# A different form of the seven-product block pair in an FFN, and a fourth pair in the first FFN

## The chip, the cores and the metric

The kernel runs on one core of one Trainium2 chip. The metric is the device time of one execution in microseconds (us); a kernel's time is the median of its runs. Engines are named as in the profile: PE is TensorE (PEld its weight loads), DVE is VectorE, ACT is ScalarE, POOL is GpSimd, SP is SyncE, which only issues loads. L433 is the line of the profile for nearly every instruction, since a helper (issue, line 430) emits them all.

## The reference

Two layers on 256 tokens of width 1024, everything in float32. Each layer is a macaron half-step FFN, a mixer (an mLSTM in layer 0, a differential attention on a shared K/V in layer 1), a second half-step FFN, and a gated per-layer embedding, each with a norm before and behind it. Four FFNs hence, of this form, with a hidden width of 2816:

```
def swiglu(x, w_in, w_out):
    gate, up = jnp.split(x @ w_in, 2, axis=-1)
    return (jax.nn.silu(gate) * up) @ w_out
...
        h = swiglu(rms_norm(x, g[0]), w_ffn_in[layer, 0], w_ffn_out[layer, 0])
        x = x + 0.5 * rms_norm(h, g[1])
...
        h = swiglu(rms_norm(x, g[4]), w_ffn_in[layer, 1], w_ffn_out[layer, 1])
        x = x + 0.5 * rms_norm(h, g[5])
```

## The kernel before, in words

The 256 tokens are two tiles of 128 (NT = 2). An FFN (function ffn) is cut into 11 items (NJ) of 256 hidden columns, gate and up together 512 columns. An item's input weight is two tiles of 128x2048 float32, 1 MB each, its output weight is one such tile. Each tile is loaded into one of NRAW = 10 buffers `wraw` and split in two (split, line 464): ACT copies the high part into one of NPART = 6 buffers `whi`, DVE subtracts to get the low part into one of NLOW = 5 buffers `wlo`. A float32 product of 128 rows is then three matmuls (mm3, line 507): high by high, high by low, low by high. So stage_in(j, t), the input product of item j for token tile t, is 24 matmuls of 128x512; hidden(j, t) makes silu(gate) times up, transposes it on PE and splits it; stage_out(j, t) adds 12 matmuls into the output sum.

A block pair (block_pair, line 718) does two items for both token tiles with 7 products of 12 matmuls where single items need 8: it is a 2x2 block scheme of the Winograd kind. Its names: src is the first item's two weight tiles (b11, b21), src2 the second's (b12, b22); xf gives four sums of the token side, s1, s2, s3 and n4 (forms, line 700). On the weight side it needs t3 = b12 + b22 and u1 = b11 + b12, which a second, accumulating transfer on POOL's queue adds to a loaded tile (load with plus), and wt2 = b11 + t3 and wt4 = b21 + wt2, which DVE adds. w11, w21, w22, wu1, wt2, wt3, wt4 are the split forms. The products in order are x0·w11, x0·w21 (together p1, hidden(0, 0)), s2·wt2, s1·wu1 (held as z5), s3·wt3, n4·w22, x1·wt4, and use(item, t, source) hands each finished sum to hidden. Here b22 is loaded by itself for w22, beside the t3 that holds it already, so a pair loads 5 tiles and accumulates 2. For a pair that follows a pair of the same FFN, t3 and u1 are loaded a pair ahead (ahead, nxt). Behind a pair come the stage_outs of the items before it.

PAIRS names the items at which pairs start: (5, 7, 9) in the first FFN, (1, 3, 5, 7, 9) in the other three, so 18 pairs; the mLSTM has 2 more. Items 3 and 4 of the first FFN are single.

The order of the work is no more than partly that of the code. The program is written down first (Notes), then a planner (play, line 267) takes for each engine the next operation by its costs, a rank from the program's order and whether the operation is marked urgent, gives the buffers, and issue emits each engine's operations in that order. On the chip every engine then works strictly in its own order and waits for semaphores.

## Time and profile before

| | |
|---|---|
| runs of the kernel | 1003.70, 1004.13, 1004.54 us; median 1004.13 |
| the profiled execution | 1002.59 us |
| its span in the trace | 1000.8 us |
| granted PE clock, mean | 0.997 |
| moved by DMA | 274.68 MB |

The span runs from the first to the last instruction in the trace; 1.8 us of the profiled time lie around it. The FFNs take, by the order of the stages, the first part (0 to about 150 us), from about 280, from about 500, and the end from about 780 us on. Busy times of engines are shares of the span; an engine that waits for a semaphore is idle in them. A matmul's listed length is modelled and reaches over the start of the next one, so the distance from start to start is what it costs.

### The profile page before, as it was taken

How to read it: one execution, taken by the hardware profiler on the slowest of the kernel's cores; microseconds unless marked ns; L12 is line 12 of the kernel's file. 1: busy time of each engine (PE TensorE's matmuls, PEld its weight loads, DVE VectorE, ACT ScalarE, POOL GpSimd, SP SyncE). 2: the span in 40 equal slices, each digit the busy share in tenths (PEclk: the TensorE clock that was granted, in tenths of full speed). 3: DMA queues.
4: the chain of work that ended last, by engine and by line, in shares of the span. 5: the costliest groups of instructions: out<-in, count | busy, mean ns of one | idle time of the engine just before them, and what ended most of it. 6: DMA issues, size and time to landing. Idle time of an engine off the chain costs nothing.

```text
span 1000.8 us, 12442 instructions
## 1 busy us (share of the span) xinstructions
PE 986.4 (99%) x4636; PEld 803.0 (80%) x4636; DVE 892.8 (89%) x909; ACT 698.6 (70%) x924; POOL 94.9 (9%) x126
## 2 busy tenths in 40 slices
PE   9999999999999999999999999999999999999997
PEld 7888888887787778888878888888888887878786
DVE  6977999799999999998799999898984999999983
ACT  7746777578756877685867767686776776757752
POOL 0010000300141000001120000001002300000010
PEclk9999999999999999999999999999999999999998
DMA  9999948765699999765699999864759899996621
GB/s 345 420 339 343 311 179 296 244 207 198 255 320 340 326 309 335 279 247 207 261 301 330 324 353 347 329 244 161 253 210 285 235 297 318 313 295 252 242 84 43
DMA packets 45859, 274.68 MB, mean 274 GB/s; under 512 B 5480, under 2 KB 5864, under 8 KB 16104
## 3 DMA queue, kind: packets, MB, share of 16 engines
q1 hardware_dynamic: 39752, 231.69, 60.2%
q0 software_dynamic: 5760, 41.95, 20.6%
q8 instruction: 36, 0.59, 0.2%
q10 hardware_dynamic: 288, 0.27, 0.1%
q14 instruction: 23, 0.19, 0.1%
HBM read 263.40 MB, written 10.49 MB: 274 GB/s over the span
## 4 chain that ended last, share of the span: by engine, by line
PE 47%; issue 2%; ACT 2%; POOL 1%; DVE 1%; DVEq 0%; POOLq 0%; ACTq 0%
PE accI L433 30%; PE accO L433 15%; PE tr L433 2%; POOL sm L433 1%; ACT sg L433 1%; DVE wlo_4r L433 0%; ACT att L433 0%; DVE wlo_2r L433 0%; ACT wraw L433 0%; ACT whi_5r L433 0%; ACT whi_0r L433 0%; DVE wraw L433 0%; DVE att L433 0%; DVE xl_5r L433 0%; DVEq L1498 0%
## 5 line engine op out<-in xcount | busy, mean ns | idle before, releaser
L433 DVE TENSOR_TENSOR wraw<-wraw,wraw 128x2048 f32<-128x2048 f32 x40 | 91.4, 2284 | 0.1
L433 ACT ACTIVATE whi_1r<-wraw 128x2048 fp32r<-128x2048 f32 (+2 forms) x49 | 72.7, 1494 | 18.2 <-PE accI L433 8.8
L433 ACT ACTIVATE whi_4r<-wraw 128x2048 fp32r<-128x2048 f32 (+1 forms) x45 | 75.4, 1684 | 11.9 <-issue 4.4
L433 ACT ACTIVATE whi_2r<-wraw 128x2048 fp32r<-128x2048 f32 (+1 forms) x48 | 79.4, 1661 | 5.5 <-issue 2.6
L433 ACT ACTIVATE whi_5r<-wraw 128x2048 fp32r<-128x2048 f32 (+1 forms) x47 | 79.2, 1694 | 5.6 <-PE accI L433 4.7
L433 ACT ACTIVATE whi_0r<-wraw 128x2048 fp32r<-128x2048 f32 (+2 forms) x48 | 74.5, 1557 | 6.8 <-PE accI L433 3.4
L433 ACT ACTIVATE whi_3r<-wraw 128x2048 fp32r<-128x2048 f32 (+1 forms) x45 | 73.6, 1647 | 3.3 <-PE accI L433 1.6
L433 ACT ACTIVATE att<-accI 128x512 f32<-128x512 f32 x80 | 47.5, 594 | 38.1 <-PE accI L433 37.8
L433 POOL DMA_DIRECT2D wraw<-in_ffn_in x36 | 32.0, 889 | 343.5 <-DMA wraw<-in_ffn_in 286.3
L433 POOL TENSOR_SCALAR sm<-sm 128x1 f32<-128x1 f32 x32 | 23.5, 735 | 308.8 <-ACT sg L433 308.8
L433 POOL TENSOR_TENSOR sm<-sm,mhalf 128x1 f32<-128x1 f32 (+2 forms) x40 | 30.7, 769 | 108.2 <-DVE sm L433 105.6
L433 ACT ACTIVATE sg<-att,sm 128x256 f32<-128x256 f32 x54 | 26.9, 502 | 16.9 <-DVE att L433 16.8
L433 ACT ACTIVATE sg<-accO 128x512 bf16<-128x512 f32 (+2 forms) x46 | 20.2, 445 | 25.0 <-PE accO L433 21.0
L433 ACT ACTIVATE sg<-accI,sm 128x256 f32<-128x256 f32 x34 | 16.0, 470 | 29.3 <-PE accI L433 27.3
L433 PEld LDWEIGHTS tr<-ident,sg 128*128 128x128 f32 x176 | 23.0, 140 | 14.6 <-DVE hl_2r L433 2.7
L433 PE MATMUL tr<-ident,sg 128*128 128x128 f32 x176 | 34.0, 274 | 0.3 <-DVE hl_2r L433 0.3
L433 DVE SCALAR_TENSOR_TENSOR wraw<-wraw,sm,wraw 128x512 f32<-128x512 f32 x32 | 22.7, 749 | 12.0 <-POOL sm L433 11.9
L433 DVE TENSOR_TENSOR att<-accI,att 128x512 f32<-128x512 f32 x40 | 27.4, 685 | 3.3 <-PE accI L433 2.9
L433 ACT ACTIVATE sg<-wraw 128x512 bf16<-128x512 f32 x32 | 20.1, 630 | 13.7 <-DVE wraw L433 9.7
L433 ACT ACTIVATE att<-accI,sm 128x512 f32<-128x512 f32 (+1 forms) x22 | 14.8, 671 | 20.8 <-PE accI L433 20.8
L433 DVE SCALAR_TENSOR_TENSOR sg<-att,sm,sg 128x256 f32<-128x256 f32 x54 | 25.7, 480 | 1.7 <-ACT sg L433 1.5
L433 DVE TENSOR_TENSOR att<-att,att 128x512 f32<-128x512 f32 (+1 forms) x33 | 22.4, 679 | 3.8 <-ACT att L433 3.6
(610 smaller groups left out, 3249.9 us busy)
## 6 DMA issues: line engine op xcount, KB each, us to landing
wraw<-in_ffn_in SPq DMA_DIRECT2D x102, 1024.0 KB, 9.4
wraw<-in_ffn_out SPq DMA_DIRECT2D x44, 1024.0 KB, 8.3
wraw<-in_ffn_in POOLq DMA_DIRECT2D x36, 1024.0 KB, 13.3
wraw<-in_mlstm_in SPq DMA_DIRECT2D x14, 1024.0 KB, 5.3
wraw<-in_ple_gate SPq DMA_DIRECT2D x8, 1024.0 KB, 5.1
wraw<-in_w_kv SPq DMA_DIRECT2D x8, 1024.0 KB, 4.8
home<-wraw SPq DMA_DIRECT2D x28, 256.0 KB, 5.1
wraw<-home SPq DMA_DIRECT2D x14, 512.0 KB, 5.4
```

The lines of the kernel that those rows point to most:

```text
L433: getattr(getattr(self.nc, eng), name)(*args, **kw)
```

## The change

NRAW goes from 10 to 9 and NLOW from 5 to 6, which takes the same room. PAIRS gives the first FFN a fourth pair, items 3 and 4; as the first pair of its FFN it has the old form, and pair (5, 6) now follows a pair. Every pair that follows another of its FFN (15 of them now) takes a new form, the branch `if ahead is not None`; the first pairs of the four FFNs and the two of the mLSTM keep the old one.

In the new form only u1 is loaded a pair ahead. The tile for t3 is loaded with b22 alone and split for w22, and then an accumulating transfer adds b12 into the same buffer, which makes it t3; so b22 isn't loaded a second time (4 loads and 2 accumulates). The products are in another order: s1·wu1 and n4·w22 first (both held in pieces, z5 and z4, one ACT copy more), then x0·w11 and x0·w21, then the stage_outs of the items before, which stood behind the pair (between, outs), and then s2·wt2, s3·wt3 and x1·wt4. In the last pair of an FFN one stage_out is kept for behind it.

```
-NRAW = 10
+NRAW = 9
 NPART = 6
-NLOW = 5
+NLOW = 6
...
-PAIRS = ((5, 7, 9),) + ((1, 3, 5, 7, 9),) * 3
+PAIRS = ((3, 5, 7, 9),) + ((1, 3, 5, 7, 9),) * 3
...
+        if ahead is not None:
+            nc.is_urgent = False
+            u1 = ahead
+            t3 = load(src2[1])
+            nc.is_urgent = True
+            w22 = parts(t3)
+            nc.gpsimd.dma_start(t3, src2[0], accum_op=ALU.add)
+            nc.is_urgent = False
+            wu1 = parts(u1)
+            b11 = load(src[0])
+            w11 = parts(b11)
+            b21 = load(src[1])
+            w21 = parts(b21)
+            nc.is_urgent = True
+            s1, s2, s3, n4 = xf() if callable(xf) else xf
+            az = acc_in()
+            times(az, s1, wu1, False)
+            z5 = held(az)
+            times(az, n4, w22, True)
+            z4 = held(az)
+            ax, ay = acc_in(), acc_in()
+            times(ax, quarter(0, 0), w11, False)
+            p1 = held(ax)
+            times(ay, quarter(0, 4), w21, False)
+            nc.vector.tensor_tensor(p1, ay, p1, op=ALU.add)
+            use(0, 0, p1)
+            if between:
+                between()
+            nc.is_urgent = False
+            wt2 = add(b11, b11, t3)
+            ahead = load(nxt[0][0], nxt[1][0]) if nxt else None
+            wt3 = parts(t3)
+            wt4 = add(b21, b21, b11)
+            nc.is_urgent = True
+            times(ax, s2, wt2, True)
+            u2 = held(ax)
+            nc.vector.tensor_tensor(u2, z4, u2, op=ALU.subtract)
+            use(1, 0, u2)
+            times(ax, s3, wt3, True)
+            u3 = held(ax)
+            nc.vector.tensor_tensor(z5, z5, u3, op=ALU.subtract)
+            use(1, 1, z5)
+            times(ax, quarter(1, 4), wt4, True)
+            use(0, 1, ax)
+            return ahead
         nc.is_urgent = False
-        t3, u1 = ahead or (load(src2[0], src2[1]), load(src[0], src2[0]))
+        t3, u1 = load(src2[0], src2[1]), load(src[0], src2[0])
...
-        ahead = (load(nxt[1][0], nxt[1][1]), load(nxt[0][0], nxt[1][0])) if nxt else None
+        ahead = load(nxt[0][0], nxt[1][0]) if nxt else None
...
             if len(item) == 2:
                 nxt = items[begin + n + 1]
-                ahead = both(item, between=late if split_begin and n == 0 else None, ahead=ahead,
-                             nxt=[win[i] for i in nxt] if len(nxt) == 2 else None)
+                between = late if split_begin and n == 0 else (lambda: outs(behind)) if ahead is not None else None
+                ahead = both(item, between=between, ahead=ahead, nxt=[win[i] for i in nxt] if len(nxt) == 2 else None)
...
-            both(item, end=True, ahead=ahead)
...
+            both(item, end=True, between=lambda: outs(behind, 1), ahead=ahead)
+            outs(behind)
```

How this moves instructions is shown at three places. In these rows a name such as wraw_3_79 is buffer 3 of `wraw`, a row "wlo<-wraw,whi" is the low half of a split, a row "wraw<-wraw,wraw" an add of two weight tiles, and "att" and "sg" rows are the small ones on held sums and hidden values.

The first place is DVE at the meeting of the first and the second pair of the fourth FFN. Before, the last row is the split of the second pair's u1 (wraw_3_79); ahead of it stand the splits of the first pair's wt4 (wraw_7_83) and of the second pair's b21 (wraw_4_80) and the add of its wt2 (wraw_0_76). The split of the first pair's wt2 lies nine rows above the first one shown:

```order
L433 TENSOR_TENSOR att_4_102<-att_4_102,att_6_104 128x512
L433 TENSOR_TENSOR wlo_1r_72<-wraw_7_83,whi_4r_69 128x2048
L433 TENSOR_TENSOR att_1_99<-accI_0_90,att_1_99 128x512
L433 SCALAR_TENSOR_TENSOR sg_0_126<-att_4_102,sm1_5_161,sg_0_126 128x256
L433 TENSOR_TENSOR wlo_3r_74<-wraw_4_80,whi_3r_68 128x2048
L433 TENSOR_TENSOR hl_0r_123<-tr_0_97,hh_0r_120 128x256
L433 SCALAR_TENSOR_TENSOR sg_1_127<-att_1_99,sm1_6_162,sg_1_127 128x256
L433 SCALAR_TENSOR_TENSOR sg_2_128<-accI_1_91,sm1_5_161,sg_2_128 128x256
L433 TENSOR_TENSOR wraw_0_76<-wraw_0_76,wraw_8_84 128x2048
L433 TENSOR_TENSOR hl_1r_124<-tr_0_97,hh_1r_121 128x256
L433 TENSOR_TENSOR att_3_101<-accI_0_90,att_3_101 128x512
L433 TENSOR_TENSOR wlo_2r_73<-wraw_3_79,whi_5r_70 128x2048
```

In the changed kernel the rows begin with the split of the first pair's wt2 (wraw_2_79) and end with that of the second pair's u1 (wraw_3_80); w22 of the second pair (wraw_1_78) is among them:

```order
L433 TENSOR_TENSOR wlo_4r_75<-wraw_2_79,whi_2r_67 128x2048
L433 TENSOR_TENSOR xl_6r_119<-att_4_102,xh_6r_112 128x512
L433 TENSOR_TENSOR wlo_1r_72<-wraw_7_84,whi_4r_69 128x2048
L433 SCALAR_TENSOR_TENSOR sg_0_126<-accI_2_92,sm1_5_161,sg_0_126 128x256
L433 TENSOR_TENSOR wlo_5r_76<-wraw_6_83,whi_0r_65 128x2048
L433 TENSOR_TENSOR wlo_4r_75<-wraw_1_78,whi_2r_67 128x2048
L433 TENSOR_TENSOR hl_0r_123<-tr_0_97,hh_0r_120 128x256
L433 TENSOR_TENSOR wlo_0r_71<-wraw_0_77,whi_5r_70 128x2048
L433 TENSOR_TENSOR wlo_2r_73<-wraw_4_81,whi_3r_68 128x2048
L433 TENSOR_TENSOR att_3_101<-att_3_101,att_6_104 128x512
L433 TENSOR_TENSOR wlo_1r_72<-wraw_3_80,whi_4r_69 128x2048
```

So from wt2 of the first pair to u1 of the second there lie seven operations on whole weight tiles (128x2048), both counted, and four small rows; before, ten and eleven. The splits of b11 and b21 and the add of wt2 of the second pair have moved behind u1, the add of the first pair's wt4 to ahead of these rows, and w22 of the second pair has come in.

The second place is DVE a little later in the same pair, before with the splits of wt2, t3 and b22, the add of wt4 (wraw_4_80) and then the first of the output weights (wraw_6_82, in two halves):

```order
L433 SCALAR_TENSOR_TENSOR sg_0_126<-att_3_101,sm1_6_162,sg_0_126 128x256
L433 TENSOR_TENSOR wlo_0r_71<-wraw_0_76,whi_0r_65 128x2048
L433 TENSOR_TENSOR wlo_1r_72<-wraw_8_84,whi_1r_66 128x2048
L433 TENSOR_TENSOR wlo_4r_75<-wraw_1_77,whi_4r_69 128x2048
L433 TENSOR_TENSOR wraw_4_80<-wraw_4_80,wraw_0_76 128x2048
L433 TENSOR_TENSOR wlo_2r_73<-wraw_6_82,whi_3r_68 128x1024
L433 TENSOR_TENSOR att_5_103<-att_5_103,att_7_105 128x512
L433 TENSOR_TENSOR wlo_2r_73<-wraw_6_82,whi_3r_68 128x1024
L433 TENSOR_TENSOR att_0_98<-accI_1_91,att_0_98 128x512
```

In the changed kernel, behind u1, come b11 (wraw_5_82), b21 (wraw_8_85), the two output weights (wraw_2_79 and wraw_7_84), and only then the add of wt2, which takes t3 from wraw_1_78:

```order
L433 SCALAR_TENSOR_TENSOR sg_1_127<-att_3_101,sm1_5_161,sg_1_127 128x256
L433 TENSOR_TENSOR wlo_3r_74<-wraw_5_82,whi_1r_66 128x2048
L433 TENSOR_TENSOR hl_2r_125<-tr_0_97,hh_2r_122 128x256
L433 SCALAR_TENSOR_TENSOR sg_2_128<-att_1_99,sm1_6_162,sg_2_128 128x256
L433 SCALAR_TENSOR_TENSOR sg_0_126<-accI_1_91,sm1_5_161,sg_0_126 128x256
L433 TENSOR_TENSOR wlo_5r_76<-wraw_8_85,whi_0r_65 128x2048
L433 TENSOR_TENSOR hl_0r_123<-tr_0_97,hh_0r_120 128x256
L433 TENSOR_TENSOR wlo_0r_71<-wraw_2_79,whi_5r_70 128x1024 x2
L433 TENSOR_TENSOR wlo_2r_73<-wraw_7_84,whi_3r_68 128x2048
L433 TENSOR_TENSOR wraw_5_82<-wraw_5_82,wraw_1_78 128x2048
```

The output weights have moved ahead of wt2, t3 and wt4, as the stage_outs have on PE; the add of wt2 stands behind six whole splits and one in two halves and eight small rows, counted from w22's. The two halves of one output weight lie in one row of the order ("x2").

The third place is POOL in the first FFN, before with its six accumulating transfers for three pairs, two by two:

```order
L433 DMA wraw_7_83<-in_ffn_in 128x2048 [waits DMAHW7_49]
L433 DMA wraw_8_84<-in_ffn_in 128x2048 [waits DMAHW0_49]
L433 DMA wraw_3_79<-in_ffn_in 128x2048 [waits DMAHW5_49,DMAHW6_49,DMAHW4_49,DVE_49]
L433 DMA wraw_4_80<-in_ffn_in 128x2048 [waits DMAHW5_49]
L433 DMA wraw_8_84<-in_ffn_in 128x2048 [waits DMAHW3_49]
L433 DMA wraw_7_83<-in_ffn_in 128x2048 [waits DMAHW4_49]
```

In the changed kernel there are eight for four pairs:

```order
L433 DMA wraw_2_79<-in_ffn_in 128x2048 [waits DMAHW3_49,DMAHW1_49,DMAHW4_49,DMAHW0_49,DVE_49]
L433 DMA wraw_3_80<-in_ffn_in 128x2048 [waits DMAHW5_49,DMAHW6_49,DMAHW1_49,DVE_49]
L433 DMA wraw_7_84<-in_ffn_in 128x2048 [waits DMAHW7_49]
L433 DMA wraw_1_78<-in_ffn_in 128x2048 [waits DMAHW1_49,DVE_49]
L433 DMA wraw_4_81<-in_ffn_in 128x2048 [waits DMAHW6_49]
L433 DMA wraw_8_85<-in_ffn_in 128x2048 [waits DMAHW7_49,DVE_49,Activation_49]
L433 DMA wraw_1_78<-in_ffn_in 128x2048 [waits DMAHW4_49]
L433 DMA wraw_4_81<-in_ffn_in 128x2048 [waits DMAHW0_49,DVE_49]
```

Of each later pair one of the two transfers, the one that makes t3, now waits for DVE to have split the tile it goes into, and stands on POOL's queue ahead of or behind the other pair's u1 as shown.

More of the change, by code (lines that the diff above doesn't have):

```diff
@@ L712, in forms, with load @@
         return [q1, q2, q3, q4]
-    def block_pair(xts, xf, src, src2, use, end=False, between=None, nxt=None, ahead=None):
-        def load(src, plus=None):
-            raw = T([P, 2048], "wraw", NRAW)
-            nc.sync.dma_start(raw, src)
-            if plus is not None:
-                nc.gpsimd.dma_start(raw, plus, accum_op=ALU.add)
-            return raw
+    def load(src, plus=None):
+        raw = T([P, 2048], "wraw", NRAW)
+        nc.sync.dma_start(raw, src)
+        if plus is not None:
+            nc.gpsimd.dma_start(raw, plus, accum_op=ALU.add)
+        return raw
+    def block_pair(xts, xf, src, src2, use, end=False, between=None, nxt=None, ahead=None):
         def parts(raw):
@@ L762, in held @@
             return c
+        if ahead is not None:
[43 more added lines that the diff above has]
+            return ahead
+        nc.is_urgent = False
+        t3, u1 = load(src2[0], src2[1]), load(src[0], src2[0])
+        b11 = load(src[0])
+        w11 = parts(b11)
+        b21 = load(src[1])
+        w21 = parts(b21)
+        wt2 = add(b11, b11, t3)
+        wu1 = parts(u1)
+        wt3 = parts(t3)
+        b22 = load(src2[1])
+        w22 = parts(b22)
+        ahead = load(nxt[0][0], nxt[1][0]) if nxt else None
+        wt4 = add(b21, b21, b11)
+        nc.is_urgent = True
         ax, ay = acc_in(), acc_in()
@@ L871, in late, with outs @@
             stage_out(0, 1)
+        def outs(todo, keep=0):
+            while len(todo) > keep:
+                stage_out(*todo.pop(0))
         def all_forms():
@@ L889, in ffn @@
                     stage_in(item[0], t)
-            for t in range(NT):
-                for i in last:
-                    stage_out(i, t)
+            outs(behind)
             last = item
@@ L908, in ffn @@
         else:
-            both(item, end=True, ahead=ahead)
-            for t in range(NT):
-                for i in last:
-                    stage_out(i, t)
+            behind = [(i, t) for t in range(NT) for i in last]
+            both(item, end=True, between=lambda: outs(behind, 1), ahead=ahead)
+            outs(behind)
             for t in range(NT):
```

13 lines of the change are left out of this document (1 added, 12 removed).

## Prediction

> **What bounds the kernel now.** I read the page first, then the windows by stretch, then the chain of waits and the timelines where a window showed a gap. The page's busy times, and one piece of the chain from the third FFN (start us, us, what):
>
> ```profile
> PE 986.4 (99%) x4636; PEld 803.0 (80%) x4636; DVE 892.8 (89%) x909; ACT 698.6 (70%) x924; POOL 94.9 (9%) x126
> 593.25 15.90 PE accI L433 x70
> ```
>
> TensorE is the bound: 99% of the span. Its unit price is in the second line: 70 matmuls of 128x512 in 15.90 us, 0.227 us each, so a product or a stage_out of 12 costs 2.72 us. VectorE (DVE) at 89% is the only other engine that can decide, and the mean hides where. Windows of 30 us (start:end, window's length, then PE, PEld, DVE, ACT, POOL busy, granted clock, DMA share, GB/s), the first two in the second FFN, one in the third, two in the fourth:
>
> ```profile
> 300.00:330.00 30.00, 28.88 (x130) 22.41 (x129) 29.61 (x31) 22.27 (x27) 4.41 (x6) 1.00 1.02 354
> 330.00:360.00 30.00, 29.38 (x131) 23.10 (x130) 30.00 (x26) 22.92 (x26) 1.72 (x2) 1.00 0.99 307
> 600.00:630.00 30.00, 30.00 (x137) 24.57 (x136) 29.89 (x22) 20.82 (x22) 1.72 (x2) 1.00 1.02 330
> 830.00:860.00 30.00, 27.67 (x124) 21.96 (x123) 29.53 (x24) 20.09 (x21) 1.74 (x2) 1.00 0.97 309
> 860.00:890.00 30.00, 30.00 (x135) 24.07 (x134) 28.54 (x22) 20.86 (x22) 1.73 (x2) 1.00 0.99 314
> ```
>
> In the pairs DVE is 95 to 100% busy and TensorE full, except at the starts of the second and fourth FFN, where PE falls short by 1.12 + 0.62 and 2.33 us while DVE is full: there DVE decides. The chain at the start of the fourth FFN, and PE's timeline in the second (in brackets the idle time before a matmul and its releaser):
>
> ```profile
> 829.82 0.69 DVE att L433
> 830.51 2.21 DVE wlo_2r L433
> 832.72 0.04 issue
> ...
> 838.28 0.61 ACT att L433
> ```
> ```profile
> 313.11 0.39 PE L433 MATMUL accI<-whi_5r,xh_2r 128*128 128x512 f32 x1
> 314.15 0.50 PE L433 MATMUL accI<-wlo_4r,xh_2r 128*128 128x512 f32 x1 [0.65 <-DVE wlo_4r L433]
> ...
> 317.17 0.38 PE L433 MATMUL tr<-ident,sg 128*128 128x128 f32 x2
> 318.02 0.50 PE L433 MATMUL accI<-whi_4r,xh_4r 128*128 128x512 f32 x1 [0.47 <-ACT att L433]
> ```
>
> The piece of 2.21 us is DVE's low part of u1 of the second pair, which TensorE stands and waits for: 0.69 + 2.21 there and 0.61 later, about 3.5 us on the chain, of which the window shows 2.33 as idle. The profiled run took 1002.59 us (span 1000.8), 1.54 less than the median 1004.13, so I work against 1002.59 and add 1.54 at the end.
>
> **The change, part by part.**
>
> *One more pair in the first FFN.* Items 3 and 4 go from 8 products to 7: 12 matmuls x 0.227 = 2.7 us less of TensorE. This holds in full only if nothing else becomes late.
>
> *What the new pair asks of the first FFN.* Two single items need 4 splits of 128x2048; a pair in the old form, which this one is, as the first of its FFN, has 7 splits and 2 adds, so 5 DVE operations more. Their price, DVE's timeline in the fourth FFN, and the room, windows of 25 us and ACT's waits for loads between 25 and 100 us (total, times, longest):
>
> ```profile
> 833.02 2.29 DVE L433 TENSOR_TENSOR wlo_0r<-wraw,whi_0r 128x2048 fp32r<-128x2048 f32 x1
> 835.23 2.29 DVE L433 TENSOR_TENSOR wlo_1r<-wraw,whi_1r 128x2048 fp32r<-128x2048 f32 x1
> ```
> ```profile
> 50.00:75.00 25.00, 25.00 (x115) 20.60 (x114) 18.03 (x15) 10.58 (x11) 3.04 (x4) 1.00 1.02 339
> 75.00:100.00 25.00, 25.00 (x114) 20.60 (x113) 19.74 (x16) 17.45 (x18) 1.80 (x3) 1.00 1.02 342
> 100.00:125.00 25.00, 25.00 (x114) 20.59 (x113) 23.98 (x19) 17.85 (x17) 0.00 (x0) 1.00 1.00 313
> ```
> ```profile
> ACT whi_4r L433 <- DMA wraw<-in_ffn_out: 0.6, 1, 0.6
> ACT whi_3r L433 <- DMA wraw<-in_ffn_in: 0.6, 1, 0.6
> ```
>
> From one start to the next is 2.20 us, so 11.0 us, and three small operations on held pieces of about 0.7 make 13. DVE idles 25 - 18.03 and 25 - 19.74, 12.2 us together, from 50 to 100. So it just about fits, and DVE will be full there. The DMA share is full too (1.02). The page's queue rows price a load:
>
> ```profile
> q1 hardware_dynamic: 39752, 231.69, 60.2%
> q0 software_dynamic: 5760, 41.95, 20.6%
> ```
>
> 60.2% of 1000.8 us over 231.69 MB is 2.6 us per MB on the 16 engines, and 20.6% over 40 accumulating MB is 5.15 us. The new pair has 5 loads and 2 accumulates against 4 loads: 2.6 + 10.3 = 12.9 us more; the three pairs behind it each drop one load, 7.8 us less. Net 5.1 us in a stage whose loads now land with hardly a wait (0.6 us on ACT, none on PE). The cost is between 0 (cover found behind the leads and in the sixth low buffer) and about 6 us (half of the 12.9 comes through before the three pairs give it back). I take 1.5, near the low end, since PE's windows there are full, 25.00, and DVE's demand exceeds its idle time by only about 1 us.
>
> *The new product order in 15 pairs.* DVE work per pair stays the same (7 splits, 2 adds, and the outs), so a pair that is not at a start gains nothing. What changes is when DVE must deliver. In the old order 7 products (19.0 us of PE) stand together and need 9 whole-tile operations of DVE (19.8 us) and the small ones; in the new one 4 products and 4 stage_outs (21.8 us) need 4 + 2 splits (13.2 us) and the small ones, and the other five (11.0 us) serve three products behind those outs. So DVE is short of time in the old order, which it makes up in the outs, and ahead in the new. The case to work is the fourth FFN (the order pieces above show it): from DVE's split of the first pair's wt2 to that of the second pair's u1. DVE's timeline has them at
>
> ```profile
> 804.59 2.28 DVE L433 TENSOR_TENSOR wlo_1r<-wraw,whi_2r 128x2048 fp32r<-128x2048 f32 x1
> ...
> 819.82 0.69 DVE L433 TENSOR_TENSOR att<-att,att 128x512 f32<-128x512 f32 x1 [0.27 <-ACT att L433]
> ...
> 825.82 0.42 DVE L433 TENSOR_TENSOR hl_0r<-tr,hh_0r 128x256 fp32r<-128x256 f32 x1
> ...
> 830.43 2.28 DVE L433 TENSOR_TENSOR wlo_2r<-wraw,whi_5r 128x2048 fp32r<-128x2048 f32 x1
> ```
>
> Before, ten whole-tile operations lie from the one to the other, both counted, and it ends at 832.6. In the changed order seven lie there with four small ones (0.4 to 0.7 each, as above), 7 x 2.20 + 2.0 = 17.4 us: it could end at 822.0, or, since the small operation at 819.82 waits for ACT and stands just ahead, at 819.82 + 0.6 + 2.2 = 822.6. TensorE wants it now first in the pair instead of third: the wait before began after 829.8, and the two products (24 matmuls, 5.4 us, and a few transposes, 0.4) go behind, so it wants it at about 824.0. That is 1.4 us early, and what follows is earlier still. The stall goes. So too in the second FFN, whose order is changed alike. No stall of that kind shows in the third FFN, so nothing is to be had there. I take away 2.0 us in the second FFN (1.74 idle in its windows, and slow restarts) and 2.8 us in the fourth (between the 2.33 idle and the 3.5 of the chain); bounds 0 and about 6.5 for both.
>
> *The sixth low buffer and the ninth raw one.* The sixth lets DVE split one tile, 2.2 us, ahead before each FFN; it is part of the term above and I count nothing beyond it. With 9 raw buffers a pair now needs 4 tiles and 2 of the outs where it needed 5 and 2 of 10: three over in both cases. I cost it at nothing; if the planner's spare one was needed, it costs in the first FFN, inside the bound of 6.
>
> *One more copy per pair* (z4 held):
>
> ```profile
> L433 ACT ACTIVATE att<-accI 128x512 f32<-128x512 f32 x80 | 47.5, 594 | 38.1 <-PE accI L433 37.8
> ```
>
> 15 x 0.594 = 8.9 us on ACT, which is 20 to 23 of 30 us busy in the pairs: hidden in ACT's idle time, 0 (8.9 if that cover were gone).
>
> *The added wait.* The sum t3 now starts only when b22 is split, and the add of wt2 waits for it on DVE, with the splits behind it queued. Landing times of the accumulates (us from issue, the median of 36; then single ones: one alone, the first and second of a pair, and the slowest):
>
> ```profile
> wraw<-in_ffn_in POOLq DMA_DIRECT2D x36, 1024.0 KB, 13.3
> wraw<-in_ffn_in POOLq DMA_DIRECT2D x1, 1024.0 KB, 9.2
> wraw<-in_ffn_in POOLq DMA_DIRECT2D x1, 1024.0 KB, 12.9
> wraw<-in_ffn_in POOLq DMA_DIRECT2D x1, 1024.0 KB, 17.9
> wraw<-in_ffn_in POOLq DMA_DIRECT2D x1, 1024.0 KB, 19.0
> ```
>
> Between b22's split and the add stand on DVE, in the fourth FFN, seven whole tiles and eight small operations, 15.4 + 3.4 = 18.8 us; in the shortest pair (third FFN) two tiles fewer and some small ones more, 14.7. So by the median the wait is 0, and at the worst 19.0 - 14.7 = 4.3. I take 0: the median is under the shortest queue, and the two accumulates of a pair now lie apart, where the 17.9 was the second of two. On GpSimd's queue the next pair's u1 stands behind t3; it is wanted only a pair later. By the Trainium skill, *DMA: Bandwidth & Descriptors*, "Anatomy of one DMA — SWDGE (gpsimd) path", such a transfer takes about 2.0 us and its bytes at 436 GB/s, an estimate of 4.4 us for 1 MiB. The trace says 13.3, three times that, and the measurement decides; by the page this wait could never show, the sum would stay, and the chance of the slower rival would fall to the forecast.
>
> The sum: -2.7 + 1.5 - 2.0 - 2.8 = -6.0; 1002.59 - 6.0 = 996.6, and with 1.54 a median of 998.1, say **998.0**.
>
> **The rivals.** *Slower: the accumulate is late.* If it lands at 19.0 where 14.7 us of DVE work cover it, DVE stands for 4.3 us at the head of its row. DVE idles some 1.5 us in 30 in a pair (28.54 of 30 from 860 to 890), so about 2.8 us a pair reach TensorE. It decides once the landing passes the queue of 14.7 to 19 us; if half of the 15 pairs are so, 7 x 2.8 = 20 us, a time of 1018, and 2 such pairs more than eat the gain of the order. For it: a full DMA share (1.02) in these stages, DVE near 100%. Against: 13.3 in the median, and fewer loads per pair. The Trainium skill has a rule that speaks for this rival: *SBUF — State Buffer*, "SBUF: two separate sides", lets GpSimd's descriptor writing be locked out by DVE in some modes, so that its DMAs starve. The row of 9.2 us, at a time of little DVE work, would fit, but that transfer was also alone on its queue, so no row here separates the two. Chance 0.12.
>
> *Only the 12 matmuls count.* DVE stays as loaded as it was, and the stall returns one pair later, or at the head of the pair, where u1 is now wanted 5.4 us earlier and my margin was 1.4 us. Then -2.7 + 1.5 = -1.2: a median of 1002.9. For it: DVE at 30.00 of 30 from 330 to 360. Against: the third FFN runs without a stall at 29.89. Chance 0.15. The same case holds "it doesn't do what it says": the stage's product is gone but the path was DVE's.
>
> *The first FFN starves.* The pair waits for its two accumulates with DMA and DVE full: -2.7 + 6 - 4.8 = -1.5, 1002.6. Chance 0.10. For it: share 1.02, waits on loads already. Against: those waits are 0.6 us.
>
> **How the numbers follow.** Forecast 0.63, late accumulate 0.12, the matmuls alone 0.15, starvation 0.10. The low end takes the bounds of the order's term and no cost in the first FFN: -2.7 - 6.5 + 0.0 = -9.2, 994.9, and half a us for the scatter of the runs: 994.4. The upper end reaches over the two middle cases to 1003.5; beyond it lies the slow rival, and a little below. A measurement of this kernel can tell about 0.2% from no change, 2 us: faster is under 1002.1, slower above 1006.1. The forecast is nearly all faster (0.62), and of the middle cases with their spread of 2 us about a third (0.09): 0.71. Two thirds of them are the same: 0.16, and the slow one with a little of the first FFN's upper tail 0.13.
>
> **What would show it.** Right: in the changed profile PE's windows at the starts of the second and fourth FFN are full, no chain piece "DVE wlo" of 2 us stands there; the first FFN from 50 to 100 has PE at 24 or more of 25 and DVE near 25; TensorE has 12 matmuls fewer; ACT's busy time is up by about 9 us; DVE shows no wait for a DMA of wraw. Wrong: DVE rows 128x2048 adds with an idle time before them released by a DMA (the late accumulate); PE idle between 52 and 80 us (starvation); or PE idle at the head of a pair released by wlo, with the stall where it was.

## The result and the profile after

The changed kernel took 1005.62 us in the median of 20 runs (1004.25 to 1008.05) beside 1003.01 for the kernel before in the same session (20 runs, 1001.78 to 1004.54). The ratio is 1.0029, 95% interval 1.0023 to 1.0035: slower by 2.9 us (2.6 between the medians), where 998.0 and a gain of 6 us had been forecast. The profiled run is the fastest of the 20, 1004.25 with a span of 1002.5 us; against the profiled run before (1002.59, span 1000.8) it is 1.7 longer, so the trace shows somewhat less of the loss than the medians do.

The page of the changed kernel, its busy times, its two large queues, and the two groups of which the prediction spoke:

```profile
PE 987.4 (98%) x4624; PEld 803.3 (80%) x4624; DVE 904.9 (90%) x917; ACT 709.1 (71%) x946; POOL 91.2 (9%) x128
...
q1 hardware_dynamic: 37736, 217.01, 56.0%
q0 software_dynamic: 6048, 44.04, 22.3%
...
L433 ACT ACTIVATE att<-accI 128x512 f32<-128x512 f32 x99 | 58.1, 595 | 77.5 <-PE accI L433 77.0
...
wraw<-in_ffn_in POOLq DMA_DIRECT2D x38, 1024.0 KB, 11.8
```

The 12 matmuls are gone, the copies have come and are hidden, the accumulates land no later than before (11.8 against 13.3). TensorE is still busy for 98% of the span, with fewer matmuls and no less time: the loss stands in idle stretches and in slower matmuls. The windows find it. Five of those that the prediction had shown of before:

```profile
50.00:75.00 25.00, 24.50 (x109) 19.65 (x108) 24.04 (x17) 20.70 (x19) 1.74 (x2) 1.00 1.02 348
100.00:125.00 25.00, 24.40 (x109) 19.50 (x108) 23.32 (x17) 20.37 (x21) 0.86 (x1) 1.00 0.93 301
300.00:330.00 30.00, 29.78 (x137) 23.69 (x136) 28.98 (x30) 24.36 (x30) 6.17 (x7) 1.00 0.99 334
330.00:360.00 30.00, 29.54 (x134) 23.88 (x133) 29.11 (x24) 21.07 (x22) 1.47 (x2) 1.00 0.96 291
830.00:860.00 30.00, 30.00 (x135) 24.19 (x134) 29.17 (x23) 19.48 (x20) 1.75 (x2) 1.00 0.95 306
```

The starts of the second and the fourth FFN are nearly full now (29.78, 29.54, 30.00 where 28.88, 29.38, 27.67 stood), as forecast. The first FFN has lost its fullness (24.50 and 24.40 of 25). But none of this is a loss of 3 us. That is in a stage whose code the change does not touch, the end of the mLSTM. Windows of before and then of after:

```profile
260.00:270.00 10.00, 10.00 (x54) 8.56 (x54) 9.26 (x20) 9.18 (x18) 1.01 (x1) 1.00 0.65 248
270.00:280.00 10.00, 10.00 (x48) 7.79 (x47) 10.00 (x11) 2.99 (x4) 1.42 (x2) 1.00 0.91 350
```
```profile
260.00:270.00 10.00, 6.77 (x32) 5.15 (x30) 9.35 (x21) 9.37 (x11) 1.92 (x1) 0.98 0.71 291
270.00:280.00 10.00, 10.00 (x42) 8.10 (x43) 8.53 (x9) 5.98 (x8) 0.00 (x0) 0.85 0.89 324
```

32 matmuls where there were 54, then a window that reads 10.00 busy and holds 42 where there were 48, at a granted clock of 0.85: a full PE column is not a PE at its pace. TensorE's timeline of the changed kernel there:

```profile
265.38 0.61 PE L433 MATMUL accO<-whi_5r,xh_4r 128*128 128x512 f32 x2
267.08 0.66 PE L433 MATMUL tr<-ident,wraw 128*128 128x128 f32 x4 [1.09 <-DVE wraw L433]
269.88 0.79 PE L433 MATMUL accI<-wlo_1r,xh_2r 128*128 128x512 f32 x1 [2.15 <-DVE wlo_1r L433]
270.48 0.63 PE L433 MATMUL accI<-whi_1r,xl_2r 128*128 128x512 f32 x1
270.90 0.63 PE L433 MATMUL accI<-whi_1r,xh_2r 128*128 128x512 f32 x1
```

Two waits for DVE, and behind them matmuls that start 0.42 us apart instead of 0.23. What DVE did meanwhile, in its timelines of before and of after (the split that TensorE wants, and the rows on the heads' norms, which have `sm` in them):

```profile
263.17 2.28 DVE L433 TENSOR_TENSOR wlo_3r<-wraw,whi_0r 128x2048 fp32r<-128x2048 f32 x1
...
268.19 1.66 DVE L433 SCALAR_TENSOR_TENSOR wraw<-accO,sm,wraw 128x256 f32<-128x256 f32 x4
```
```profile
264.07 0.88 DVE L433 SCALAR_TENSOR_TENSOR wraw<-accO,sm,wraw 128x256 f32<-128x256 f32 x2
...
266.33 1.29 DVE L433 TENSOR_TENSOR wraw<-wraw,att 128x512 f32<-128x512 f32 x2
267.55 2.28 DVE L433 TENSOR_TENSOR wlo_1r<-wraw,whi_1r 128x2048 fp32r<-128x2048 f32 x1
```

Before, the split stood ahead of these norm rows, now behind them. Some thirty-five us earlier stands the first sign of it: ACT at the head of its row waits for a load of the second mLSTM pair, and DVE idles behind ACT. ACT and DVE of before, then of after:

```profile
232.50 1.92 ACT L433 ACTIVATE whi_1r<-wraw 128x2048 fp32r<-128x2048 f32 x1 [2.23 <-DMA wraw<-in_mlstm_in]
...
234.93 0.69 DVE L433 TENSOR_TENSOR att<-att,att 128x512 f32<-128x512 f32 x1 [0.84 <-ACT att L433]
```
```profile
231.57 1.92 ACT L433 ACTIVATE whi_1r<-wraw 128x2048 fp32r<-128x2048 f32 x1 [3.04 <-DMA wraw<-in_mlstm_in]
...
234.00 0.69 DVE L433 TENSOR_TENSOR att<-att,att 128x512 f32<-128x512 f32 x1 [2.97 <-ACT att L433]
```

DVE has lost 2.1 us more there than before. The two waits of ACT aren't for the same load: before it is for the pair's fourth, now for its third (b11). SP's rows for that third load, of before and of after:

```profile
214.03 0.33 SPq L433 DMA_DIRECT2D wraw<-in_mlstm_in  x1
```
```profile
220.27 0.33 SPq L433 DMA_DIRECT2D wraw<-in_mlstm_in  x1
```

Just before it SP has waited 7.3 us for a split on DVE, which sets a raw buffer free. Before the change SP makes such a stop (6.7 us) one load later. The third load comes 6.2 us later, as if a buffer were missing.

To see what each stage won or lost, the matmul of the same number is looked up in both traces (the n-th from the start; behind the first FFN, the n-th from the end) and the starts are subtracted; worked out from the records, in us. Where the two orders differ it isn't the same matmul, which moves a row by some tenths, at most 0.8. Each trace is one execution. The last column belongs to experiment 13, below:

```
stage that ends here       start before   after - before   exp. 13 - before
kernel's first 30 us            30.2          -0.9              -0.6
first FFN                      163.3          -1.3              -0.9
mLSTM, second pair's products  261.2          -1.1              +0.7
mLSTM, end                     273.9          +4.2              +0.7
second FFN, pairs              383.1          +1.6              -0.3
third FFN                      685.9          +3.0              +1.5
attention                      758.5          +5.1              +3.6
fourth FFN, its start          848.5          +1.8              +0.3
end                            993.1          +1.7              -0.1
```

So: first FFN -0.4, end of the mLSTM +5.3, second FFN -2.6, the stretch with the third FFN +1.4, attention +2.1, the start of the fourth FFN -3.3.

Attention's 2 us need rows of their own, for no wait shows there. They lie in the small score matmuls, which contract 64 rows. TensorE's timeline of before, then of after, without the single matmuls that stand between:

```profile
732.65 2.16 PE L433 MATMUL accO<-wraw,wraw 64*128 64x128 f32 x32
```
```profile
735.22 1.26 PE L433 MATMUL accO<-wraw,wraw 64*128 64x128 f32 x16
...
736.73 1.16 PE L433 MATMUL accO<-wraw,wraw 64*128 64x128 f32 x8
...
738.13 1.16 PE L433 MATMUL accO<-wraw,wraw 64*128 64x128 f32 x8
```

The last 32 of them stood together before; now they stand as 16, 8 and 8, with a matmul of another kind between. A group of 8 takes as long as 16 do in one row elsewhere (1.09 us from its start to the start of what follows). From start to start the 96 score matmuls of the stage take 6.4 us before and 7.6 after, and the 8 others that stand among them (128x256) 0.9 and 1.5: 1.9 us in all. From the first score matmuls to the end of attention every kernel below with the new order of products has lost 1.7 to 2.0 us against before, whatever its buffers, and every one with the old order 0.1 or less. The change does not touch attention's code either: the planner arranges the whole program, and a change upstream has moved a group downstream.

### The profile page after: what moved, and what is told of

Its sections match the earlier page's. It is cut to its first block, busy times and chain, and to the rows that moved or that the text cites. A ratio compares the mean times of both kernels' runs of the same rounds, so it can differ in the third digit from the quotient of the medians.

```text
span 1002.5 us, 12373 instructions
## 1 busy us (share of the span) xinstructions
PE 987.4 (98%) x4624; PEld 803.3 (80%) x4624; DVE 904.9 (90%) x917; ACT 709.1 (71%) x946; POOL 91.2 (9%) x128
## 5 line engine op out<-in xcount | busy, mean ns | idle before, releaser
L433 DVE TENSOR_TENSOR wlo_4r<-wraw,whi_2r 128x2048 fp32r<-128x2048 f32 (+1 forms) x25 | 48.5, 1943 | 1.8 <-ACT whi_2r L433 1.8
L433 DVE TENSOR_TENSOR wlo_5r<-wraw,whi_0r 128x2048 fp32r<-128x2048 f32 (+1 forms) x23 | 46.2, 2007 | 2.5 <-ACT whi_0r L433 2.5
L433 DVE TENSOR_TENSOR wlo_2r<-wraw,whi_3r 128x2048 fp32r<-128x2048 f32 (+1 forms) x23 | 44.0, 1914 | 3.9 <-ACT whi_3r L433 3.9
L433 DVE TENSOR_TENSOR wlo_3r<-wraw,whi_3r 128x2048 fp32r<-128x2048 f32 (+1 forms) x23 | 46.1, 2004 | 0.7 <-ACT whi_3r L433 0.7
L433 DVE TENSOR_TENSOR wlo_4r<-wraw,whi_4r 128x2048 fp32r<-128x2048 f32 (+1 forms) x23 | 45.9, 2005 | 0.5 <-ACT whi_4r L433 0.5
L433 DVE TENSOR_TENSOR wlo_5r<-wraw,whi_5r 128x2048 fp32r<-128x2048 f32 (+1 forms) x23 | 46.1, 2005 | 0.1
L433 DVE TENSOR_TENSOR wlo_1r<-wraw,whi_1r 128x2048 fp32r<-128x2048 f32 (+2 forms) x26 | 44.2, 1708 | 0.0
L433 DVE TENSOR_TENSOR wlo_1r<-wraw,whi_4r 128x2048 fp32r<-128x2048 f32 (+1 forms) x23 | 43.7, 1913 | 0.0
L433 DVE TENSOR_TENSOR wlo_0r<-wraw,whi_0r 128x2048 fp32r<-128x2048 f32 (+2 forms) x20 | 37.1, 1859 | 2.4 <-ACT whi_0r L433 2.4
L433 DVE TENSOR_TENSOR wlo_0r<-wraw,whi_5r 128x2048 fp32r<-128x2048 f32 (+1 forms) x20 | 37.0, 1856 | 0.3 <-ACT whi_5r L433 0.3
## 6 DMA issues: line engine op xcount, KB each, us to landing
wraw<-in_ffn_in POOLq DMA_DIRECT2D x38, 1024.0 KB, 11.8
```

Source lines behind the costliest of these rows:

```text
L433: getattr(getattr(self.nc, eng), name)(*args, **kw)
```

## The experiments

Theory A, with which the experiments began: the gap in the mLSTM comes from the buffers (ten raw tiles to nine), not from the new order of products; the order's gain is real. Its rivals: the new order or the fourth pair moved DVE's row; or the gap only moves if one cures it where it is (D in the expectations). Ratios are to the kernel before in the same session, with 95% intervals.

**1, buffers alone.** The kernel before with

```
-NRAW = 10
+NRAW = 9
-NLOW = 5
+NLOW = 6
```

> The kernel before with only the buffer counts of the change: NRAW 9, NLOW 6; old pairs, three pairs in the first FFN. Theory A (the loss comes from the ninth raw buffer: with it the planner orders the end of the mLSTM otherwise, DVE's norm of the second token tile comes late, and TensorE runs out of covering products at about 260 to 275 us; in the changed kernel that cost 5.2 us, and the attention 2.2): the stall is here too, 4 to 7 us slower than before, ratio about 1.005. The FFN starts keep their stalls, or lose 1 us by the sixth low buffer. Theory B (the new pair form, or the fourth pair's shift of the timing, makes the loss, and the buffer counts by themselves do nothing): within 1 us of before, no gap over 1 us between 255 and 280.

Measured: 1008.97 us, 1.0066 [1.0041, 1.0090]. The same gap, with none of the new order, in TensorE's timeline of this kernel:

```profile
270.45 0.66 PE L433 MATMUL tr<-ident,wraw 128*128 128x128 f32 x4 [1.12 <-DVE wraw L433]
273.25 0.69 PE L433 MATMUL accI<-wlo_0r,xh_4r 128*128 128x512 f32 x1 [2.15 <-DVE wlo_0r L433]
273.74 0.63 PE L433 MATMUL accI<-whi_0r,xl_4r 128*128 128x512 f32 x1
```

So the buffers are enough to make it. They do more: the expectation had the FFN starts keep their stalls, but the start of the fourth FFN is nearly full here too, with the old order of products:

```profile
830.00:860.00 30.00, 29.53 (x132) 22.90 (x131) 29.20 (x25) 21.69 (x25) 1.72 (x2) 1.00 0.94 301
```

Before it was 27.67. From 330 to 360 it is worse, 27.73 where 29.38 stood. **2, the ninth raw buffer alone** (`NRAW = 9`, five low ones) separates the two sizes:

> The kernel before with NRAW 9 alone, NLOW stays 5. Theory A: as with both counts, the stall at the mLSTM's end of about 5 us, 5 to 8 us slower, since nothing is won at the FFN starts. Theory B: within 1 us of before. If the stall needs the sixth low buffer, it is absent here.

Measured: 1017.97, 1.0149 [1.0132, 1.0167]. The raw buffer makes the gap and more: with five low buffers the starts of the FFNs stall too (17.79 of 20 us busy from 340 to 360, 28.16 of 30 from 850 to 880). The sixth low buffer gives back 9 us of it.

**3, the new order with the old buffers** (the changed kernel with `NRAW = 10`, `NLOW = 5`), and **4, that with three pairs** in the first FFN (`PAIRS = ((5, 7, 9),) + ...`):

> The changed kernel with the old buffer counts, NRAW 10 and NLOW 5. Theory A: no stall at the mLSTM's end, the gains at the starts of the second and fourth FFN stay (2 and 3 us), the first FFN gives about nothing (2.7 won, 2.4 lost): 4 to 6 us faster than before, ratio about 0.995. Theory B: as the changed kernel, 2 to 3 us slower than before. A third way: the new order needs the sixth low buffer, and the stalls at the FFN starts come back: within 1 us of before.

> The new pair form alone: the changed kernel with the old buffer counts and three pairs in the first FFN. Theory A: the starts of the second and fourth FFN are won, and the first FFN, with no fourth pair, neither wins 2.7 nor loses 2.4: 4 to 6 us faster than before. Theory B, where the form is to blame: slower than before by 2 us or more. Beside the run with the fourth pair it prices that pair by itself: by theory A within 1 us of it, by the forecast's 1.5 us for the first FFN about 1 us slower than it.

Measured: 1008.34, 1.0052 [1.0040, 1.0064], and 1007.36, 1.0043 [1.0030, 1.0057]. The gap is gone, as theory A has it, but its time was wrong: the kernel got slower, not faster. Windows over the end of the mLSTM, the second FFN and the fourth in experiment 3:

```profile
250.00:300.00 50.00, 49.63 (x237) 40.45 (x237) 45.73 (x60) 33.08 (x55) 12.04 (x10) 1.00 0.81 271
300.00:350.00 50.00, 48.35 (x218) 38.02 (x217) 49.55 (x48) 39.49 (x46) 3.55 (x5) 1.00 0.98 332
...
850.00:900.00 50.00, 48.23 (x216) 38.56 (x215) 47.17 (x37) 35.62 (x34) 3.46 (x4) 1.00 0.89 253
```

49.63 where the changed kernel has 46.31, but 48.35 and 48.23 where it has 49.32 and 50.00. The new order needs the new pools: with the old ones TensorE waits for low halves from DVE at 315.84, 389.43, 828.43 and 887.38 us (0.69, 1.31, 1.15 and 1.31), partly later in the FFN than the stalls that the order took away; the window of 850 to 900 was full before the change. That it is the sixth low buffer which is missing fits these waits, but here both counts went back, so it isn't shown apart in the new order; in the old one it is (experiments 1 and 2). The prediction had the buffer as part of the order's term and counted nothing for it alone; the term is nothing without it.

**5, the load hurried.** The changed kernel, in which the last sum of the second mLSTM pair counts as urgent for the planner:

```
-    def block_pair(xts, xf, src, src2, use, end=False, between=None, nxt=None, ahead=None):
+    def block_pair(xts, xf, src, src2, use, end=False, between=None, nxt=None, ahead=None, hurry=False):
...
+        nc.is_urgent = hurry
...
-        block_pair(xts, all_forms(), a["mlstm_in"][4], a["mlstm_in"][5], opened)
+        block_pair(xts, all_forms(), a["mlstm_in"][4], a["mlstm_in"][5], opened, hurry=True)
```

**8, the same flag in experiment 1's kernel** (old order, nine and six buffers):

> The changed kernel with one flag: in the second mLSTM pair the add and the split of wt4 are marked urgent, so that DVE splits it ahead of the second token tile's norm. Theory C (now: the pairs give what was forecast, and the loss stands at three other places, the end of the mLSTM with 5.3 us through the ninth raw buffer, the attention with 2.2 and the third FFN with 1.0 through the new form): the gap of 3.5 us and the slow matmuls behind it between 264 and 273 us are gone, 4 to 5.5 us faster than the changed kernel, so 1.5 to 2.5 us faster than before, ratio 0.9975 to 0.9985. Rival D (the gap only moves, since DVE is late there in any case with nine raw buffers): as the changed kernel, ratio 1.002 to 1.004.

> The kernel before with the new buffer counts (9 and 6) and the same flag on the mLSTM's wt4: old form, three pairs. Beside the same kernel without the flag, which took 6.6 us more than before, it tells whether the flag is worth the whole gap in another program too, and beside the mended changed kernel it prices the new form with the new buffers. Theory C: the gap of 5.3 us is gone, 1 to 2 us slower than before, ratio 1.001 to 1.002; so the new form with its fourth pair is worth 3 to 4 us in the same buffers. Rival D: ratio 1.006 as without the flag.

Measured: 1006.21, 1.0033 [1.0021, 1.0045], and 1010.88, 1.0074 [1.0062, 1.0086]. Neither is cured. In experiment 5 the gap stands elsewhere:

```profile
234.69 0.39 PE L433 MATMUL accI<-whi_3r,xl_0r 128*128 128x512 f32 x1
237.00 0.62 PE L433 MATMUL accI<-whi_2r,xh_2r 128*128 128x512 f32 x1 [1.93 <-ACT att L433]
237.42 0.63 PE L433 MATMUL accI<-wlo_2r,xh_2r 128*128 128x512 f32 x1
```

The rival was right: the planner's urgency moves the gap, it does not make room. ACT's wait for the load has grown to 5.25 us there.

**6 and 7, the fourth pair.** The changed kernel with three pairs, and the kernel before with four (`PAIRS = ((3, 5, 7, 9),) + ...`, old order, old buffers):

> The changed kernel with three pairs in the first FFN, everything else new. It prices the fourth pair with the new buffers. Theory C, by the distance between the two traces at 136 us: the pair wins 2.7 and loses 2.4 to waits between 59 and 106 us, so this kernel is 0 to 1 us slower than the changed one, ratio to before 1.003 to 1.004. Rival E (the fourth pair is where the loss is: full DMA, late accumulates): this kernel is faster than the changed one by 2 us or more, at or below before.

> The kernel before with the fourth pair alone: old form, old buffers. The forecast's terms give -2.7 + 1.5 = -1.2 us, ratio 0.999. Theory C (the waits in the first FFN eat the pair whatever the form, as they do in the changed kernel with the old buffers, where it cost 1.0 us net): between 0 and 1.5 us slower, ratio 1.000 to 1.0015; no stall at the mLSTM's end.

Measured: 1006.95, 1.0033 [1.0021, 1.0045], and 1008.35, 1.0053 [1.0040, 1.0066]. In the changed kernel the fourth pair is worth 0 to 1 us of its 2.7 (1.0033 against 1.0029, within the noise). In the kernel before it costs 5 us, in the new order with the old pools 1 us (experiments 3 and 4). Its windows in the kernel before:

```profile
50.00:100.00 50.00, 47.31 (x209) 37.64 (x207) 46.72 (x34) 34.97 (x32) 3.46 (x4) 1.00 1.02 332
100.00:150.00 50.00, 48.93 (x221) 39.15 (x221) 42.73 (x37) 34.30 (x34) 2.08 (x3) 1.00 0.86 316
150.00:200.00 50.00, 49.20 (x226) 39.12 (x225) 46.50 (x42) 34.18 (x45) 9.49 (x13) 1.00 0.81 268
```

2.69 + 1.07 + 0.80 = 4.6 us of TensorE idle, the longest wait 1.45 us for a held piece from ACT. The kernel before has 50.00 in all three; the changed kernel 49.50, 49.40 and 50.00. So the new order and the sixth buffer do carry the fourth pair better than the old ones do, but not for nothing.

**9 and 11, the mLSTM's pairs in the new order too** (with four pairs, and with three), since these two pairs were left in the old one:

```
-        block_pair(xts, all_forms(), a["mlstm_in"][2], a["mlstm_in"][3], value)
+        u1 = load(a["mlstm_in"][2][0], a["mlstm_in"][3][0])
+        u1s = [block_pair(xts, all_forms(), a["mlstm_in"][2], a["mlstm_in"][3], value, ahead=u1,
+                          nxt=(a["mlstm_in"][4], a["mlstm_in"][5]))]
...
-        block_pair(xts, all_forms(), a["mlstm_in"][4], a["mlstm_in"][5], opened)
+        block_pair(xts, all_forms(), a["mlstm_in"][4], a["mlstm_in"][5], opened, ahead=u1s[0])
```

> The changed kernel with both mLSTM pairs in the new form too (the flag that marked wt4 urgent is gone again): each loads one tile less and holds one raw buffer less, so with nine raw buffers the splits of the second pair come earlier. Theory F (the gap at the mLSTM's end is ACT and DVE late behind loads that wait for a raw buffer, so that only fewer buffers in use or more buffers cure it, not another order of the same work): the gap of 3.5 us and the slow matmuls behind it are gone, 4 to 6 us faster than the changed kernel, ratio to before 0.9965 to 0.999. Rival G (the token side of the mLSTM, the norm chain of the second tile, makes the gap, whatever the weights do): as the changed kernel, ratio 1.002 to 1.004.

> As the kernel with both mLSTM pairs in the new form, with three pairs in the first FFN: the fourth pair priced once more, without the gap. Theory: the pair is worth nothing in these buffers (2.7 won, 2.4 lost, as the trace of the changed kernel beside that with three pairs showed), so the two kernels agree within 1 us. By the forecast's 1.5 us for the first FFN this one is 1.2 us slower.

Measured: 1009.38, 1.0060 [1.0048, 1.0073], and 1010.34, 1.0070 [1.0057, 1.0083]. No cure: from 250 to 300 us TensorE is busy 46.41 of 50 (changed kernel 46.31). This theory fell. Whether the new form sets a raw buffer free at the time when it is wanted was not looked at.

**10 and 12, ten raw buffers and six low ones**, paid for with one of the six high ones so that the room stays the same (`NRAW = 10`, `NLOW = 6`, `NPART = 5`), in the changed kernel and in experiment 9's:

> The changed kernel with ten raw and six low buffers, paid for with one buffer of the high part (NPART 5 in place of 6); the mLSTM in its old form. Theory F: with ten raw buffers the gap at the mLSTM's end is gone as in the two kernels that kept ten, ratio 0.997 to 1.000, if five high buffers do in the FFNs; if they don't, new waits of TensorE for ACT's high parts stand in the pairs, and the time is at or above before. Rival G: the gap stays.

> Both together: mLSTM pairs in the new form, ten raw, six low and five high buffers. If raw buffers are what the first FFN and the mLSTM lack, this is the fastest of all, 0.5 to 2 us faster than the one with nine raw buffers. If five high buffers are too few, ACT's high parts are late in the pairs and it is slower than that one.

Measured: 1027.30, 1.0247 [1.0229, 1.0264], and 1029.11, 1.0256 [1.0242, 1.0270]. Five high buffers are far too few, so these two say nothing on the mLSTM.

**13, 14 and 15, a raw buffer back without touching a pool.** In the mLSTM the residual x is reloaded into a raw buffer (at 194 us before, at 206 in the changed kernel) and first read behind the output product, near 294. Experiment 13 is the changed kernel with that reload behind the second pair:

```
-        gbc = load_gbc(a["norm_g"][l, 3])
+        gbc = load_gbc(a["norm_g"][l, 3], late=True)
...
         block_pair(xts, all_forms(), a["mlstm_in"][4], a["mlstm_in"][5], opened)
+        load_x()
```

Here `load_gbc(..., late=True)` leaves out the load of x, and `load_x()` makes it. 14 is experiment 1's kernel with this edit, 15 the kernel before with it, the control:

> The changed kernel, but in the mLSTM the reload of x, which holds a raw buffer from 195 us on and is first read behind the output product near 294 us, is issued only behind the second block pair. If the second pair's loads come late because a raw buffer is missing there, the buffer set free brings the fifth load (issued 209.97, over 19.23 us) forward by 1 to 3 us, ACT's wait at its head (3.04 us) falls to 2 or less, the 5.2 us at the end of the mLSTM shrink to 0 to 2, and the time is 1000.5 to 1002.5. If what holds the pair up is the loads' place in SP's row or the bandwidth, and not the buffer, the gap stays and the time is 1005 to 1006.5; if the reload now comes too late, a new wait stands at the output product near 294 us and the time is 1006 or more.

> The kernel before with nine raw buffers and six low ones, as once already measured at 1.0066 of before, and with the same late reload of x. If the missing raw buffer makes the gap, 4 to 5 us come back and the time is within 0.25% of the kernel before (1002 to 1005.5); if not, it stays at 1.005 to 1.008 of it (1008 to 1011).

> The kernel before with the late reload of x alone, the control. With ten raw buffers none is missing in the mLSTM (ACT waits 2.23 us, DVE 0.84), so the reload buys at most 1 us: 1002 to 1003.5, a ratio of 0.999 to 1.001. If it is by itself worth 3 us or more, the gain of the other two kernels says nothing on the ninth raw buffer.

Measured: 1003.76, 1.0003 [0.9992, 1.0014]; 1005.28, 1.0025 [1.0012, 1.0038]; and 1004.20, 1.0007 [0.9999, 1.0016]. The edit is worth 2.6 us in the changed kernel and 4.1 in the old order with the same pools, and nothing where ten raw buffers are (15 is, if anything, 0.7 us slower). Experiment 13 fell short of its expected 1000.5 to 1002.5 us, 14 lies within its range, and 15 is 0.7 above its times but within its ratio. ACT's first wait and DVE's rows at the end of the mLSTM in experiment 13:

```profile
226.11 1.92 ACT L433 ACTIVATE whi_1r<-wraw 128x2048 fp32r<-128x2048 f32 x1 [1.38 <-DMA wraw<-in_mlstm_in]
...
263.89 2.28 DVE L433 TENSOR_TENSOR wlo_1r<-wraw,whi_1r 128x2048 fp32r<-128x2048 f32 x1
...
268.90 1.66 DVE L433 SCALAR_TENSOR_TENSOR wraw<-accO,sm,wraw 128x256 f32<-128x256 f32 x4
```

The split stands ahead of the norms again, as before, and TensorE waits for neither. The window of 250 to 300 us in the changed kernel, in experiment 1, and in 13 and 14 (nine raw buffers in all four; x late in the last two):

```profile
250.00:300.00 50.00, 46.31 (x216) 37.65 (x215) 46.12 (x58) 31.55 (x50) 8.99 (x9) 0.97 0.82 275
```
```profile
250.00:300.00 50.00, 46.29 (x215) 37.55 (x215) 45.75 (x60) 32.28 (x48) 9.85 (x8) 0.97 0.77 269
```
```profile
250.00:300.00 50.00, 49.79 (x238) 40.33 (x237) 46.51 (x62) 34.28 (x56) 12.04 (x10) 1.00 0.83 280
```
```profile
250.00:300.00 50.00, 49.30 (x234) 39.78 (x233) 46.39 (x61) 33.31 (x56) 12.43 (x9) 1.00 0.81 271
```

SP issues the pair's third load at 213.00 in 13 and at 214.19 in 14, as before the change (214.03); in experiment 1 it was 222.13. That settles what the gap is: a raw buffer missing in the mLSTM. Not settled is by which of two ways it works, since both changed together: the load that lands late at run time (ACT's 3.04 us against 1.38 for that third load), or the order that the planner, short of a buffer, gave DVE's row. Not all of it came back in the time: the table above has 13 at 0.7 instead of 4.2 behind the mLSTM, and at -0.1 instead of 1.7 at the end, for a new wait of 2.15 us stands at the start of its second FFN.

What each part of the change does in which stage can be read from these traces together. Worked out as in the table above, us against before, between matmuls that are of the same kind in the traces or nearly so; the second row gives the stretch by the trace of before:

```
                                  mLSTM   second FFN   third FFN   attention   fourth FFN
                                212-294      294-481     514-686     709-758      812-949
changed kernel                     +4.8         -1.8        +1.2        +1.9         -3.2
1, buffers alone                   +6.3         +0.6        +2.1        +0.1         -1.7
4, new order alone                 -0.1         +1.5        +0.9        +2.0         +0.6
13, changed kernel, x late         +1.4         -0.7        +1.5        +1.9         -3.2
14, buffers alone, x late          +1.3         +0.8        +1.8        +0.1         -1.3
15, before, x late                 +1.0         -0.4         0.0         0.0         +1.6
```

The mLSTM loses 4.8 to 9.2 us in all eight kernels with nine raw buffers and the early reload, and 0.2 or less, either way, in the three with ten and otherwise the old pools (3, 4 and 7). The fourth FFN gains 1.7 by the buffers alone and nothing by the order alone, and 3.2 by both. The third FFN loses by either. The +1.6 of experiment 15, where nothing of the FFN was touched, is taken up in the last section: so much can differ between two executions.

No kernel tried beats the one before; experiment 13 equals it.

## Why the prediction was wrong, point by point

**The step that failed** is the one on the ninth raw buffer: "three over in both cases. I cost it at nothing; if the planner's spare one was needed, it costs in the first FFN, inside the bound of 6." It counted the tiles of an FFN pair. But the pool serves the whole program, and in the mLSTM the gains, x, the values, the room for the heads' outputs and the loads of the pairs hold raw buffers side by side. There the tenth was needed: 5.3 us, shown by experiments 1, 2, 13 and 14, and by 3, 4 and 7, which keep ten and have no gap. Nor does the count hold for every pair: the first pairs of the FFNs and the two of the mLSTM keep the old form, 5 tiles and 2, and have two over of nine and not three. The bound was for the wrong stage, so the range did not hold it: its upper end was 1003.5, and 1005.62 was measured.

**The order's term** was right in place and, for order and pools together, near in size: -2.0 forecast and -2.6 found in the second FFN (-1.8 by the later table), -2.8 and -3.3 in the fourth. DVE's stretch from the one split to the other in the fourth FFN, worked out as 18.0 us, took 17.9, and TensorE doesn't wait for its end. But the order is not the whole cause: the buffers alone fill the start of the fourth FFN to 29.53 of 30 and win 1.7 there (experiment 1). Part of the second FFN's gain may lean on the gap ahead of it, in which DVE can get ahead: in experiment 13, without the gap, that FFN gains 1.0; but there the new wait of 2.15 us stands in the same stretch, so this was not tried apart. What the term hid is its condition: with the old pools (experiments 3 and 4) it is gone. The change's buffer sizes are thus one trade. The low buffer that the order needs is paid for with the raw one that the mLSTM needs.

**The fourth pair**: the 12 matmuls (-2.7) are there, and the cost, taken as 1.5 of a range of 0 to 6, was 2.3 (1.1 of it idle, 24.50 and 24.40 of 25; the rest was not followed up). What is left is 0.4 us. In the kernel before the cost is near 8 (experiment 7: 5.3 us slower, with the 2.7 gained), above the upper bound, though that is a case that was not forecast.

**"A pair that is not at a start gains nothing"** was taken as nothing lost either. From the end of the second FFN's pairs to the end of the third FFN 1.4 us are lost, of which only one wait of 0.41 us shows as idle, and in attention 2.1. This belongs to a term that the sum did not have: the planner lays out the whole program anew. Attention's part is tied to the new order by all the traces; why the planner breaks up that group was not tried. The third FFN's part comes with the buffers too (experiments 1 and 14).

**The copies and the added wait** were right at nothing. ACT's copies went from 80 to 99 and PE waits for none of them longer than 0.5 us; DVE shows no wait for a DMA of a raw tile in the whole trace. The landing time of 4.4 us that was worked out from the Trainium skill, *DMA: Bandwidth & Descriptors*, "Anatomy of one DMA — SWDGE (gpsimd) path", is off again (median 11.8), but nothing hung on it, since the cover of 14.7 to 18.8 us holds either. So the slower rival as written, the late accumulate, is false, though the slower side came out. "Only the 12 matmuls count" and "the first FFN starves" are false too: the order's gain is there, and the first FFN gave back most of its product without starving.

Summed: -0.9 (start) - 0.4 + 0.2 + 5.3 - 2.6 + 1.4 + 2.1 - 3.3 - 0.1 = 1.7 us between the two traces. The forecast had -6.0. Of the difference of 7.7, the mLSTM is 5.5 (0.2 + 5.3) and attention with the third FFN 3.5; the smaller gain of the first FFN takes 0.8 more; the start, which was not forecast and whose cause was not looked for, gives 0.9 back, the larger order's term 1.1, the end 0.1.

## What to carry to other kernels

A pool that is made smaller is costed where the most of its tiles are held at once, over the whole program, and not in the stage that the change is for: list which tiles live in it in each stage, and look for the load that already waits at the head of an engine's row (here ACT's 2.23 us before the change). A buffer can be won back by moving a load closer to its first reader, which cost nothing clear of noise here and gave 2.6 to 4.1 us. And where a planner arranges the whole program, lay the traces side by side matmul by matmul in every stage, for it may pay elsewhere for what it wins here.

## What the runs showed of the hardware

After some idle stretches TensorE's matmuls of 128x512 started 0.42 us apart instead of 0.23, for 3.4 us: in the changed kernel behind two waits of 1.09 and 2.15 us, in experiment 5 from 237.00 on, behind one of 1.93. The granted clock reads 0.51 from 269.7 to 273.1 in the one and 0.50 from 237.2 to 240.6 in the other. The length of the wait alone does not decide it: in experiment 13 a wait of 2.15 us was followed by the usual pace.

```profile
304.78 0.50 PE L433 MATMUL accI<-whi_2r,xh_2r 128*128 128x512 f32 x1 [2.15 <-DVE sg L433]
...
305.80 0.40 PE L433 MATMUL accI<-whi_2r,xh_2r 128*128 128x512 f32 x1
306.03 0.40 PE L433 MATMUL accI<-wlo_2r,xh_2r 128*128 128x512 f32 x1
```

Nor do the program and its waits: at the start of the fourth FFN the kernel before and experiment 15 have the same two waits of 1.06 and 1.03 us, and 3.4 us from the second on hold 15 matmuls in the one and 8 in the other:

```profile
832.80:836.20 3.40, 3.40 (x15) 2.85 (x16) 3.40 (x3) 1.31 (x3) 0.00 (x0) 1.00 0.99 333
```
```profile
833.40:836.80 3.40, 3.40 (x8) 2.75 (x9) 3.40 (x3) 0.68 (x1) 0.00 (x0) 0.50 0.94 325
```

Eight matmuls at 0.2 us more add 1.6 us, so a wait of 2 us can cost near 4, and one trace can differ from another by 1.6 us at such a place; what makes the difference stays open. The other surprise is the price of attention's 64-row matmuls, which depends on their neighbours: 6.4 us for the 96 where the last 32 stand together, 7.6 where they are broken up into 16, 8 and 8.
